# Lo parts of twelve projection weight units made in the first feed-forward stage, kept in DRAM and loaded by both projection stages

## The chip, the core and the metric

The kernel runs on one core of a Trainium2 chip. A core has a matrix engine (TensorE, PE in the profile, with its weight loads as PEld), a vector engine (VectorE, DVE), a scalar engine with activation functions (ScalarE, ACT), a general engine (GpSimd, POOL) and a sync engine (SyncE, SP) that here only issues DMA transfers. Data is worked on in on-chip memory, matmuls write into PSUM banks, and weights come from DRAM. The metric is the device time of one execution in microseconds; lower is better. Before the change three runs gave 2329.94 to 2330.9 us, with a median of 2329.94 us.

## What is computed

The reference is a two-layer decoder trunk over 528 positions (16 learned ones and 512 tokens) of width 1024, in float32. Only the first layer's mixer matters to the change:

```python
h = h + 0.5 * swiglu(rms_norm(h, g[0]), ffn_w_in[i, 0], ffn_w_out[i, 0])
hn = rms_norm(h, g[1])
h = h + rwkv7_time_mix(hn, ...)        # layer 0; layer 1 has sparse attention here
h = h + 0.5 * swiglu(rms_norm(h, g[2]), ffn_w_in[i, 1], ffn_w_out[i, 1])

def rwkv7_time_mix(h, mix, w_r, w_k, w_v, ...):
    xx = jnp.pad(h, ((0, 0), (1, 0), (0, 0)))[:, :-1] - h
    xm = h[None] + xx[None] * mix[:, None, None, :]
    xr, xw, xk, xv, xa, xg = xm[0], xm[1], xm[2], xm[3], xm[4], xm[5]
    r = xr @ w_r
    k = xk @ w_k
    v = xv @ w_v
    w_log = -jax.nn.softplus(-(w0 + jnp.tanh(xw @ w1) @ w2)) - 0.5
    a = jax.nn.sigmoid(a0 + (xa @ a1) @ a2)
    ...
```

So each projection multiplies its own mix of the normed input with that of the position before it.

## The kernel before

**Split products.** Every large product is made of three matmuls on rounded operands (`mm3`): a weight block and an input are each split into a hi part (rounded to the matmul's format) and a lo part (the rest), and hi by hi, hi by lo and lo by hi are added up in PSUM.

**Weights.** All weight blocks (128 by 128, and some wider) lie in DRAM in one array, `wall`, in the order of their use, packed in units of up to 1024 columns, eight blocks. The class `Weights` streams them. For each unit SP loads 512 KB into one of four `wraw` buffers, ScalarE makes the hi part (`whi`, by an activation that copies and rounds), and VectorE makes the lo part (`wlo`, by `tensor_sub` of raw and hi, called a split below). There are four buffers each of `wraw`, `whi` and `wlo`. `take` hands a block to the matmul code; at each call it first calls `split` for the unit two ahead, and in the second half of a unit it calls `round` for the unit three ahead. `prefetch` does the same from other places. One order of calls in the code is the order on each engine's queue, which is worked off in that order.

**Stages.** Positions are worked on in two ranges, A (0 to 272, padded to 288 in the mixer) and B (272 to 528). `STAGES` lists the order of the weights, and with it of the stages: feed-forward A (the first stage), projection A, feed-forward B, output projection A, projection B, and so on. A weight matrix used for both ranges is streamed twice, so both projection stages load the same units and split them anew. In the first stage 67 units are used.

**The projection stage.** `proj` makes mixes: for each of six uses i and eight channel blocks d, VectorE makes `tb` = hn + xx * mix, ScalarE rounds it into `xm_hi`, GpSimd subtracts it from `tb` into `xm_lo`. For the first use (i = 2, the k projection) VectorE also normalizes the block (`ynat`), takes the difference with the position before (`bu`), and, in range A only, copies the last position into `hnlast` for range B. There are four `tb` buffers (shared with other code) and twelve pairs of `xm_hi` and `xm_lo`. The order of matmuls is that of `proj_steps`: a first pass of `wk` over all d into four PSUM banks (32 blocks), a second pass for the other four banks with the sixteen blocks of the two low-rank factors (`lw`, `la`) among them, then `wv` and `wr`. The mixes are issued in the order k, w, a, v, r, g, each as soon as a buffer is free in program order. `evac` copies a finished bank to `BKV`. The first twelve units of the stage hold `wk`, `lw`, `la` and the first sixteen blocks of `wv`.

**Work beside.** The recurrence of the mixer (preparation, inverse, scan) runs as chains of small operations that a static planner, `run` with the prices of the class `Clock`, threads between the main matmuls. Its decisions are made when the program is built.

Of the kernel before, what the change touches and what calls it, by code (L numbers as in the profile page):

```python
# [10 lines left out]
F32 = mybir.dt.float32  # L11
F32R = mybir.dt.float32r
I32 = mybir.dt.int32
AF = mybir.ActivationFunctionType
# [120 lines left out]
def ao_blocks():  # L135
    return [blk("ao", d, m) for m in range(DT) for d in range(DT)]


STAGES = (("ffn", 0, 0), ("proj",), ("ffn", 0, 0), ("out",), ("proj",), ("ffn", 0, 1), ("out",), ("ffn", 1, 0),
          ("ffn", 0, 1, (0, 2)), ("idx",), ("ffn", 0, 1, (2, 4)), ("kvq",), ("ffn", 1, 0), ("ao",), ("idx",), ("kvq",),  # L140
          ("ffn", 1, 1), ("ao",), ("ffn", 1, 1))


def plan(stages=STAGES):


    f = {"ffn": ffn_blocks, "proj": proj_blocks, "out": out_blocks, "idx": idx_blocks, "kvq": kvq_blocks,
         "ao": ao_blocks}
    units, width = [], 0
    for name, *args in stages:  # L150
        for piece in f[name](*args):
            w = piece[3] - piece[2]
            if not units or width + w > (512 if len(units) < 3 else 1024):
                units.append([])
                width = 0
            units[-1].append((piece, width))
            width += w
    return units


def unit_width(u):
    (_, _, c0, c1), at = u[-1]
    return at + c1 - c0


def pack(units, mats):

    wall, c = np.empty(128 * sum(unit_width(u) for u in units), np.float32), 0
    for u in units:
        w = unit_width(u)  # L170
        t = wall[c:c + 128 * w].reshape(128, w)
        for (key, k, c0, c1), at in u:
            t[:, at:at + c1 - c0] = mats[key][k * 128:(k + 1) * 128, c0:c1]
        c += 128 * w
    return wall


class Weights:


    def __init__(self, nc, pool, wall, units, raw_bufs, bufs, ahead):
        self.nc, self.pool, self.wall, self.units = nc, pool, wall, units
        self.raw_bufs, self.bufs, self.ahead = raw_bufs, bufs, ahead
        self.flat = [(u, p) for u, unit in enumerate(units) for p in unit]
        self.start = 128 * np.concatenate([[0], np.cumsum([unit_width(u) for u in units])])
        self.pos = self.nraw = self.nhi = self.nlo = 0
        self.raw, self.hi, self.lo = {}, {}, {}

    def load(self):

# [20 lines left out]
    def split(self, last):  # L211

        while self.nlo <= min(last, len(self.units) - 1):
            self.round(self.nlo)
            r = self.raw.pop(self.nlo)
            w = r.shape[1]
            lo = self.pool.tile([128, 1024], F32R, name="wlo", bufs=self.bufs)
            self.nc.vector.tensor_sub(lo[:, :w], r, self.hi[self.nlo][:, :w].bitcast(F32))
            self.lo[self.nlo] = lo
            self.nlo += 1  # L220

    def prefetch(self, n):

# [3 lines left out]
    def take(self, piece):  # L227
        u, (p, at) = self.flat[self.pos]
        assert p == piece, (self.pos, p, piece)
        self.split(u + self.ahead)  # L230
        if at >= 512:
            self.round(u + self.ahead + 1)
        self.pos += 1
        s = slice(at, at + piece[3] - piece[2])
        return self.hi[u][:, s], self.lo[u][:, s]
# [195 lines left out]


@with_exitstack
def trunk(ctx, tc, wall, units, h0, vec, cstd, gqk, out, stop=None, gap=0.0, share=400.0, slack=200.0, fulls={}):
    clock = Clock()
    nc = Core(tc.nc, clock)
    @contextmanager
# [11 lines left out]
    W = Weights(nc, wpool, wall, units, raw_bufs=4, bufs=4, ahead=2)  # L449

    h = consts.tile([128, DT, T], F32, name="h")

# [12 lines left out]
    cst = {}  # L465
# [331 lines left out]
    hnlast = consts.tile([128, DT, 1], F32, name="hnlast")  # L797
# [4 lines left out]
    def proj(R, norm, sp, core, XB):  # L802

        r, n, pad, nch = R.r, R.n, R.pad, R.nch
        n0 = n - pad
        hn2 = [core.tile([128, 4, 1 + 288], F32, name="ynat", bufs=2) for _ in range(2)]
        hn = [hn2[d // 4][:, d % 4] for d in range(DT)]
# [5 lines left out]
                nc.vector.tensor_copy(hn2[i][:, :, 0:1], hnlast[:, 4 * i:4 * i + 4])  # L813
        if r not in norm.rstd:
            spread = norm.stat(r)
            W.prefetch(1)
            spread()
        xx = [core.tile([128, 4, 288], F32, name="bu", bufs=2) for _ in range(2)]
        if pad:
# [24 lines left out]
        def mixes(k):  # L844
            while k and queue and free[0]:
                i, d = queue.pop(0)
                if i == 2:
                    norm.apply(d, r, hn[d][:, 1:1 + n0])
                    nc.vector.tensor_sub(xx[d // 4][:, d % 4, :n0], hn[d][:, 0:n0], hn[d][:, 1:1 + n0])
                mix(i, d)  # L850
                if i == 2 and pad:
                    nc.vector.tensor_copy(hnlast[:, d], hn[d][:, n0:n0 + 1])
                free[0] -= 1
                k -= 1

# [55 lines left out]
        for kind, *st in proj_steps():  # L911
            if kind == "d":
# [15 lines left out]
            elif kind == "lora":  # L928
                key, d = st
# [13 lines left out]
            else:  # L943
                d = st[0]
# [906 lines left out]
```

## Time and profile before

| what | value |
|---|---|
| median of three runs | 2329.94 us |
| span of the profiled execution | 2326.1 us |
| instructions | 49383 |
| busy share of the span: PE, DVE, ACT, POOL | 97%, 73%, 54%, 8% |
| chain that ended last: PE, DVE, ACT, issue, DMA | 82%, 12%, 3%, 2%, 1% |
| splits (`wlo`) | 658 of 1235 ns mean |
| roundings of weights (`whi`) | 658 of 1051 ns mean |
| bytes moved | 355.98 MB, mean 153 GB/s |

The runs give device time alone; the profiled execution is one further execution, whose span from the first to the last instruction is 2326.1 us, 3.84 us less than the median of the runs. All rows name line 341, since a helper records every operation, so rows are told apart by their tiles: `acc<-xm_hi,whi` is a matmul of a mix with a weight's hi part into an `acc` bank. In the rows of a timeline the first number is the start in us, the second the busy time, a trailing xN says that N instructions in a row were merged, and a bracket says how long the engine was idle before and what ended that.

The first stage runs to about 212 us, projection A starts its matmuls at 221 us, and projection B its mixes at 660 us.

### The profile page before, as it was taken

What the parts mean: (1) busy time and instruction counts of PE and PEld (TensorE: products, weight loads), DVE (VectorE), ACT (ScalarE), POOL (GpSimd) and SP (SyncE); (2) the same over time, 40 slices, a digit from 0 to 9 for tenths busy, and PEclk for the clock granted to TensorE, in tenths of its full rate; (3) what the DMA queues carried; (4) which work ended last, traced back from release to release, by engine and by line L of the source; (5) the groups of instructions that cost most, each with busy time, mean ns of one, the idle gap of its engine ahead of it and who ended that gap; (6) DMA issues with size and microseconds to landing.
All of it is one profiled execution on the core that took longest, in us unless ns stands there. A gap on an engine that the chain in (4) does not pass through costs nothing.

```text
span 2326.1 us, 49383 instructions
## 1 busy us (share of the span) xinstructions
PE 2252.8 (97%) x20106; PEld 2171.0 (93%) x20106; DVE 1702.0 (73%) x3283; ACT 1264.8 (54%) x2137; POOL 174.5 (8%) x226
## 2 busy tenths in 40 slices
PE   8998899999989999999999999999999999999999
PEld 8998889998988899998999999989999899989999
DVE  7666888856887976577565757887656997876665
ACT  5444664466447634655444545457754647675543
POOL 0001521010033111000000000000000000000000
PEclk9999999999989999999999999999999999999999
DMA  6553334532434445234555555444454553434554
GB/s 233 177 172 124 128 128 152 193 113 66 146 128 145 156 153 166 83 128 149 182 172 173 181 166 181 162 160 149 137 182 148 168 175 117 151 109 156 185 183 144
DMA packets 101555, 355.98 MB, mean 153 GB/s; under 512 B 11552, under 2 KB 15728, under 8 KB 101328
## 3 DMA queue, kind: packets, MB, share of 16 engines
q1 hardware_dynamic: 99120, 347.91, 45.8%
q0 software_dynamic: 2208, 4.92, 0.8%
q8 instruction: 158, 2.59, 0.5%
q14 instruction: 69, 0.57, 0.1%
HBM read 348.51 MB, written 4.28 MB: 152 GB/s over the span
## 4 chain that ended last, share of the span: by engine, by line
PE 82%; DVE 12%; ACT 3%; issue 2%; DMA 1%; POOL 0%; SPq 0%; DVEq 0%; ACTq 0%; POOLq 0%
PE acc L341 70%; PE bg L341 8%; PE ry L341 3%; DVE wlo L341 3%; DVE tb L341 2%; ACT whi L341 1%; DMA wraw<-wall 1%; DVE ynat L341 0%; DVE rel L341 0%; DVE st L341 0%; DVE h L341 0%; DVE m L341 0%; DVE bu L341 0%; DVE pr L341 0%; DVE nst L341 0%
## 5 line engine op out<-in xcount | busy, mean ns | idle before, releaser
L341 ACT ACTIVATE whi<-wraw 128x1024 fp32r<-128x1024 f32 (+1 forms) x658 | 688.6, 1051 | 425.9 <-PE acc L341 272.0
L341 DVE TENSOR_TENSOR wlo<-wraw,whi 128x1024 fp32r<-128x1024 f32 (+1 forms) x658 | 810.5, 1235 | 148.8 <-ACT whi L341 147.9
L341 PE MATMUL acc<-hid_hi,whi 128*128 128x256 f32 (+1 forms) x1408 | 409.1, 291 | 4.6 <-DVE h L341 3.5
L341 PE MATMUL acc<-hid_lo,whi 128*128 128x256 f32 (+1 forms) x1408 | 399.9, 284 | 0.8 <-DVE hid_lo L341 0.8
L341 PE MATMUL acc<-hid_hi,wlo 128*128 128x256 f32 (+1 forms) x1408 | 400.0, 284 | 0.0
L341 PE MATMUL acc<-xa_hi,whi 128*128 128x256 f32 (+1 forms) x1088 | 310.6, 285 | 1.9 <-ACT xa_hi L341 1.9
L341 PE MATMUL acc<-xa_hi,wlo 128*128 128x256 f32 (+1 forms) x1088 | 309.0, 284 | 2.7 <-DVE wlo L341 2.7
L341 PE MATMUL acc<-x_hi,whi 128*128 128x272 f32 (+1 forms) x1024 | 302.8, 296 | 8.4 <-ACT whi L341 6.4
L341 PE MATMUL acc<-xa_lo,whi 128*128 128x256 f32 (+1 forms) x1088 | 308.2, 283 | 0.1
L341 PE MATMUL acc<-x_hi,wlo 128*128 128x272 f32 (+1 forms) x1024 | 294.6, 288 | 0.4 <-DVE wlo L341 0.4
L341 PE MATMUL acc<-x_lo,whi 128*128 128x272 f32 (+1 forms) x1024 | 294.2, 287 | 0.0
L341 PEld LDWEIGHTS acc<-hid_hi,whi 128*128 128x128 f32 x1408 | 265.7, 189 | 9.9 <-issue 4.3
L341 PEld LDWEIGHTS acc<-hid_lo,whi 128*128 128x128 f32 x1408 | 267.1, 190 | 1.3 <-DVE hid_lo L341 1.2
L341 PEld LDWEIGHTS acc<-hid_hi,wlo 128*128 128x128 f32 x1408 | 266.0, 189 | 0.0
L341 PE MATMUL acc<-xb_hi,whi 128*128 128x256 f32 x752 | 214.0, 285 | 0.0
L341 PE MATMUL acc<-xb_hi,wlo 128*128 128x256 f32 x752 | 211.3, 281 | 0.0
L341 PE MATMUL acc<-xb_lo,whi 128*128 128x256 f32 x752 | 211.3, 281 | 0.0
L341 PEld LDWEIGHTS acc<-xa_hi,wlo 128*128 128x128 f32 x1088 | 205.6, 189 | 3.8 <-DVE wlo L341 3.8
L341 PEld LDWEIGHTS acc<-xa_hi,whi 128*128 128x128 f32 x1088 | 205.8, 189 | 3.2 <-ACT xa_hi L341 2.1
L341 PEld LDWEIGHTS acc<-x_hi,whi 128*128 128x128 f32 x1024 | 195.1, 191 | 14.1 <-ACT whi L341 6.4
L341 PEld LDWEIGHTS acc<-xa_lo,whi 128*128 128x128 f32 x1088 | 205.8, 189 | 0.3 <-DVE xa_lo L341 0.3
L341 PEld LDWEIGHTS acc<-x_hi,wlo 128*128 128x128 f32 x1024 | 194.9, 190 | 1.0 <-DVE wlo L341 1.0
(309 smaller groups left out, 4376.5 us busy)
## 6 DMA issues: line engine op xcount, KB each, us to landing
wraw<-wall SPq DMA_DIRECT2D x643, 512.0 KB, 3.4
wraw<-wall SPq DMA_DIRECT2D x10, 438.0 KB, 3.3
out<-h SPq DMA_DIRECT2D x8, 256.0 KB, 2.3
h<-h SPq DMA_DIRECT2D x2, 512.0 KB, 7.9
ynat<-L POOLq DMA_DIRECT2D x2, 512.0 KB, 4.4
T<-ynat POOLq DMA_DIRECT2D x2, 512.0 KB, 4.8
gm<-T POOLq DMA_DIRECT2D x4, 224.0 KB, 7.0
L<-gm POOLq DMA_DIRECT2D x12, 64.0 KB, 2.1
```

Of the source, the lines that this page charges most:

```text
L341: r = f(*args, **kw)
```

## The change

`plan` now also gives an order of units with kinds. From the ninth unit of the first stage on (index 8), behind every fourth unit, one of the first twelve units of the projection is put in, of kind "save": it is loaded, rounded and split like any other, no matmul uses it, and its lo part is stored to a DRAM tile. In both projection stages the first twelve units are of kind "again": raw is loaded and rounded as before, but VectorE makes no split; SP loads the stored lo part into a `wlo` buffer instead. `back` issues these loads, three units ahead of the unit in use. While a save unit is among the next three, `take` looks one unit further ahead. Units are made to begin with the projection stage and to end with it.

Two smaller edits are in `proj`. `prefetch` at the head of projection A reaches three units ahead instead of one. The eight copies of the last position, by VectorE for each d, become two copies by ScalarE for four d each.

```diff
+SAVED, SAVE_FROM, SAVE_EVERY = 12, 8, 4
@@ plan
+    saved = {p + i: i for p in projs for i in range(SAVED)}
+    order, early = [], 0
+    for u, unit in enumerate(units):
+        order.append((u, "again" if u in saved else "use", saved.get(u)))
+        if early < SAVED and u >= SAVE_FROM and (u - SAVE_FROM) % SAVE_EVERY == 0:
+            order.append((projs[0] + early, "save", early))
+            early += 1
@@ split
-            self.round(self.nlo)
-            r = self.raw.pop(self.nlo)
+            u = self.nlo
+            self.round(u)
+            self.back(u)
+            r = self.raw.pop(u)
             w = r.shape[1]
-            lo = self.pool.tile([128, 1024], F32R, name="wlo", bufs=self.bufs)
-            self.nc.vector.tensor_sub(lo[:, :w], r, self.hi[self.nlo][:, :w].bitcast(F32))
-            self.lo[self.nlo] = lo
+            if self.kind[u] != "again":
+                lo = self.pool.tile([128, 1024], F32R, name="wlo", bufs=self.bufs)
+                self.nc.vector.tensor_sub(lo[:, :w], r, self.hi[u][:, :w].bitcast(F32))
+                self.lo[u] = lo
+            if self.kind[u] == "save":
+                d = self.saved[self.key[u]] = self.dram.tile([128, 1024], F32, name=f"lo{self.key[u]}")
+                self.nc.sync.dma_start(d, lo.bitcast(F32))
             self.nlo += 1
+
+    def back(self, last):
+
+        for u in range(self.nback, min(last + 1, len(self.units))):
+            if self.kind[u] == "again":
+                self.lo[u] = self.pool.tile([128, 1024], F32R, name="wlo", bufs=self.bufs)
+                self.nc.sync.dma_start(self.lo[u].bitcast(F32), self.saved[self.key[u]])
+            elif u > self.nlo:
+                return
+            self.nback = u + 1
@@ take
-        self.split(u + self.ahead)
+        n = self.ahead + ("save" in self.kind[u + 1:u + 4])
+        self.split(u + n)
+        self.back(u + 3)
         if at >= 512:
-            self.round(u + self.ahead + 1)
+            self.round(u + n + 1)
@@ proj
-            W.prefetch(1)
+            W.prefetch(3)
@@ mixes
-                if i == 2 and pad:
-                    nc.vector.tensor_copy(hnlast[:, d], hn[d][:, n0:n0 + 1])
+                if i == 2 and pad and d % 4 == 3:
+                    nc.scalar.activation(hnlast[:, d - 3:d + 1], hn2[d // 4][:, :, n0:n0 + 1], AF.Copy)
```

On VectorE, at the start of projection A, this stood before, from the normed block of d = 3 to the mix of d = 4:

```order
L341 SCALAR_TENSOR_TENSOR ynat<-h,vecs,rstd 128x272
L341 TENSOR_TENSOR bu<-ynat 128x272
L341 SCALAR_TENSOR_TENSOR tb<-bu,vecs,ynat 128x288
L341 COPY hnlast<-ynat 128x1
L341 TENSOR_TENSOR wlo<-wraw,whi 128x1024
L341 SCALAR_TENSOR_TENSOR ynat<-h,vecs,rstd 128x272
L341 TENSOR_TENSOR bu<-ynat 128x272
L341 SCALAR_TENSOR_TENSOR tb<-bu,vecs,ynat 128x288
```

Now it reads as follows from d = 6 to the end of the twelve units; the mixes of all later uses up to the low-rank result (llo) are one row of 29, the eighth mix of the first use among them:

```order
L376 SCALAR_TENSOR_TENSOR ynat<-h,vecs,rstd 128x272
L376 TENSOR_TENSOR bu<-ynat 128x272
L376 SCALAR_TENSOR_TENSOR tb<-bu,vecs,ynat 128x288
L376 SCALAR_TENSOR_TENSOR ynat<-h,vecs,rstd 128x272
L376 TENSOR_TENSOR bu<-ynat 128x272
L376 SCALAR_TENSOR_TENSOR tb<-bu,vecs,ynat 128x288 x29
L376 TENSOR_TENSOR llo<-ta,lhi 128x288
L376 TENSOR_TENSOR wlo<-wraw,whi 128x1024 x2
```

No split and no hnlast copy is left there; the order of the mixes among themselves is what it was. The same holds for projection B.

On SP, where before only raw loads stood (76 in a row, up to the constant `prod` of the preparation), the raw loads and the loads of stored lo parts now take turns around the start of projection A (the names lo_N are the DRAM tiles, in order of the units):

```order
L376 DMA wraw<-wall 128x1024 x14
L376 DMA wlo<-lo_380 128x1024
L376 DMA wraw<-wall 128x1024
L376 DMA wlo<-lo_575 128x1024
L376 DMA wraw<-wall 128x1024
L376 DMA wlo<-lo_730 128x1024
L376 DMA wraw<-wall 128x1024 x2
L376 DMA wlo<-lo_868 128x1024
L376 DMA wlo<-lo_1010 128x1024
L376 DMA wraw<-wall 128x1024
L376 DMA wlo<-lo_1158 128x1024
L376 DMA wraw<-wall 128x1024
```

The first three lo loads stand in the queue ahead of the last raw loads that the first stage issues.

On VectorE in the first stage, at the eviction of its first four banks (ta and tb from acc), this stood before:

```order
L341 TENSOR_TENSOR ss<-ss,tb 128x256
L341 TENSOR_TENSOR wlo<-wraw,whi 128x1024
L341 TENSOR_TENSOR ss<-ss,tb 128x256
L341 TENSOR_TENSOR ta<-acc,rstd 128x272
L341 TENSOR_TENSOR tb<-acc,rstd 128x272
```

and now this, with the first of the twelve added splits ahead of the eviction:

```order
L376 TENSOR_TENSOR ss<-ss,tb 128x256
L376 TENSOR_TENSOR wlo<-wraw,whi 128x1024 x2
L376 TENSOR_TENSOR ss<-ss,tb 128x256
L376 TENSOR_TENSOR ta<-acc,rstd 128x272
L376 TENSOR_TENSOR tb<-acc,rstd 128x272
```

More of the change, by code (lines that the diff above doesn't have):

```diff
@@ L148, in plan @@
          "ao": ao_blocks}
-    units, width = [], 0
+    units, width, projs = [], 1024, []
     for name, *args in stages:
+        if name == "proj":
+            projs.append(len(units))
+            width = 1024
         for piece in f[name](*args):
@@ L157, in plan @@
             width += w
-    return units
+        if name == "proj":
+            width = 1024
+    saved = {p + i: i for p in projs for i in range(SAVED)}
[5 more added lines that the diff above has]
+            early += 1
+    assert early == SAVED and order[-1][0] == len(units) - 1
+    return units, order
 def unit_width(u):
@@ L178, with __init__ @@
 class Weights:
-    def __init__(self, nc, pool, wall, units, raw_bufs, bufs, ahead):
-        self.nc, self.pool, self.wall, self.units = nc, pool, wall, units
+    def __init__(self, nc, pool, dram, wall, plan, raw_bufs, bufs, ahead):
+        units, order = plan
+        self.nc, self.pool, self.dram, self.wall = nc, pool, dram, wall
+        self.units, self.kind, self.key = [units[u] for u, _, _ in order], [o[1] for o in order], [o[2] for o in order]
         self.raw_bufs, self.bufs, self.ahead = raw_bufs, bufs, ahead
[L184 to L187, printed above, removed]
+        self.flat = [(i, p) for i, unit in enumerate(self.units) if self.kind[i] != "save" for p in unit]
+        start = 128 * np.concatenate([[0], np.cumsum([unit_width(u) for u in units])])
+        self.start = [start[u] for u, _, _ in order]
+        self.pos = self.nraw = self.nhi = self.nlo = self.nback = 0
+        self.raw, self.hi, self.lo, self.saved = {}, {}, {}, {}
     def load(self):
@@ L433, in trunk @@
 @with_exitstack
-def trunk(ctx, tc, wall, units, h0, vec, cstd, gqk, out, stop=None, gap=0.0, share=400.0, slack=200.0, fulls={}):
+def trunk(ctx, tc, wall, plan, h0, vec, cstd, gqk, out, stop=None, gap=0.0, share=400.0, slack=200.0, fulls={}):
     clock = Clock()
@@ L447, in trunk @@
     ctx.enter_context(tc.manual_schedule())
-    W = Weights(nc, wpool, wall, units, raw_bufs=4, bufs=4, ahead=2)
+    W = Weights(nc, wpool, dram, wall, plan, raw_bufs=4, bufs=4, ahead=2)
     h = consts.tile([128, DT, T], F32, name="h")
@@ L1840 @@
     arrays, mats = lay_out(inputs)
-    units = plan()
-    arrays["wall"] = pack(units, mats)
+    p = plan()
+    arrays["wall"] = pack(p[0], mats)
     nc = bacc.Bacc("TRN2", target_bir_lowering=False, num_devices=1)
@@ L1846 @@
     with tile.TileContext(nc) as tc:
-        trunk(tc, ap["wall"], units, ap["h0"], ap["vec"], ap["cst"], ap["gqk"], out)
+        trunk(tc, ap["wall"], p, ap["h0"], ap["vec"], ap["cst"], ap["gqk"], out)
     r = run_bass_kernel_spmd(nc, [arrays], core_ids=[0])
```

## The prediction

> **What bounds the kernel now.** I read the time by stretches first, for the share of TensorE, then TensorE's waits in the stretches where its count of matmuls falls, then the engines' rows in order of time there. In the rows below the columns are the stretch, its length, and for each engine its busy time with the number of instructions; then the granted clock, the DMA share and GB/s.
>
> ```profile
> 10.00:20.00 10.00, 9.84 (x76) 9.62 (x76) 7.86 (x12) 7.80 (x16) 0.00 (x0) 1.00 1.05 397
> 100.00:110.00 10.00, 10.00 (x82) 10.00 (x81) 6.44 (x11) 4.48 (x6) 0.00 (x0) 1.00 0.57 188
> 220.00:230.00 10.00, 8.53 (x49) 8.05 (x49) 9.62 (x21) 3.17 (x6) 4.45 (x4) 0.73 0.15 47
> 230.00:240.00 10.00, 6.86 (x37) 5.52 (x37) 9.62 (x17) 4.40 (x8) 5.41 (x5) 0.95 0.29 96
> 240.00:250.00 10.00, 10.00 (x69) 10.00 (x68) 10.00 (x11) 6.45 (x13) 7.75 (x8) 0.88 0.53 173
> 250.00:260.00 10.00, 9.66 (x72) 9.42 (x71) 10.00 (x9) 5.27 (x10) 9.75 (x9) 1.00 0.14 52
> 260.00:270.00 10.00, 5.91 (x35) 5.67 (x34) 9.45 (x11) 6.49 (x15) 7.43 (x8) 0.83 0.47 157
> 430.00:440.00 10.00, 10.00 (x87) 10.00 (x87) 9.53 (x18) 4.22 (x7) 0.00 (x0) 1.00 0.65 210
> 690.00:700.00 10.00, 10.00 (x86) 10.00 (x86) 10.00 (x11) 6.26 (x12) 9.64 (x10) 1.00 0.24 82
> 700.00:710.00 10.00, 5.55 (x35) 5.34 (x35) 8.91 (x11) 5.93 (x14) 7.79 (x9) 0.83 0.40 131
> ```
>
> In a feed-forward stage (430) TensorE is full and sets the time, though VectorE is busy for 9.53 of 10 us. In the first part of both projection stages (220 to 270, and up to 710) it is the other way round: the count falls to between 35 and 49 matmuls in four of these stretches, at a clock of 0.73 to 0.95, while VectorE is at 8.9 to 10. TensorE's real pace is read from the full rows: 72 matmuls in 9.66 us is 0.134 us in projection A, 86 in 10 is 0.116 us in projection B.
>
> Its waits, in the first stage (212 to 285 us) and then the second (590 to 735 us):
>
> ```profile
> PE acc L341 <- ACT BKV L341: 4.1, 1, 4.1
> PE acc L341 <- POOL xm_lo L341: 3.2, 5, 1.0
> ```
>
> ```profile
> PE acc L341 <- ACT BKV L341: 4.5, 1, 4.5
> ```
>
> It hardly waits for a lo part of the weights. It waits for mixed inputs (xm_lo), and once in each stage for ScalarE to empty the four banks of the second `wk` pass, which the first `wv` step needs. That eviction stands behind 29 rounded mixes (xm_hi) in ScalarE's order. So the chain is: VectorE makes a mix (tb), ScalarE rounds it, GpSimd subtracts; the four tb buffers come free when GpSimd is done. The splits delay that chain; that is how they cost time.
>
> **What the change takes from projection A.** VectorE in order of time, two splits among mixes:
>
> ```profile
> 226.18 1.21 DVE L341 TENSOR_TENSOR wlo<-wraw,whi 128x1024 fp32r<-128x1024 f32 x1
> 227.31 1.05 DVE L341 SCALAR_TENSOR_TENSOR ynat<-h,vecs,rstd 128x272 f32<-128x272 f32 x1
> ...
> 245.95 5.01 DVE L341 SCALAR_TENSOR_TENSOR tb<-bu,vecs,ynat 128x288 f32<-128x288 f32 x5
> 250.88 1.83 DVE L341 TENSOR_TENSOR wlo<-wraw,whi 128x1024 fp32r<-128x1024 f32 x1
> 252.64 5.06 DVE L341 SCALAR_TENSOR_TENSOR tb<-bu,vecs,ynat 128x288 f32<-128x288 f32 x5
> ```
>
> ```profile
> L341 DVE COPY hnlast<-ynat 128x1 f32<-128x1 f32 x8 | 1.1, 143 | 0.0
> ```
>
> A split takes 227.31 - 226.18 = 1.13 us of VectorE. GpSimd's first and eighth subtraction, the latter beside a split:
>
> ```profile
> 220.99 1.04 POOL L341 TENSOR_TENSOR xm_lo<-tb,xm_hi 128x288 fp32r<-128x288 f32 x1 [215.30 <-ACT xm_hi L341]
> ...
> 237.10 1.29 POOL L341 TENSOR_TENSOR xm_lo<-tb,xm_hi 128x288 fp32r<-128x288 f32 x1 [0.87 <-ACT xm_hi L341]
> ```
>
> First eight mixes: two splits stand ahead of the eighth, 2.3 us; of the eight hnlast copies I count 0.3 of 1.1 us, since neighbours overlap; the eighth subtraction loses its company, 0.25. It ends at 238.4 - 2.9 = 235.5 us. The two hnlast instructions that ScalarE gets instead hide in its idle time (3.17 busy of 10).
>
> The next 21 mixes: from 245.95 to 252.64, five mixes and one split took 6.69 us; without the split 5.55, or 1.11 a mix. I keep that pace, in which VectorE and GpSimd still slow each other; GpSimd's own 1.04 is the other end, worth 1.2 us over 17 mixes. Twelve mixes fit the buffers. TensorE has 22 matmuls left after the eighth, then 24 of the second pass before the first buffers come free: 235.5 + 46 x 0.134 = 241.7, while subtraction 12 ends at 239.9. With 0.4 for a rounding that is a gap of 2.2. Subtraction 25 ends at 235.5 + 17 x 1.11 + 2.2 = 256.6; its buffer takes mix 29, 1.0 us, at 257.6. Then ScalarE's row:
>
> ```profile
> 265.06 0.44 ACT L341 ACTIVATE xm_hi<-tb 128x288 fp32r<-128x288 f32 x1 [0.52 <-DVE tb L341]
> 265.41 1.04 ACT L341 ACTIVATE whi<-wraw 128x1024 fp32r<-128x1024 f32 x1
> 266.36 1.29 ACT L341 ACTIVATE BKV<-acc 128x288 f32<-128x288 f32 x4
> ```
>
> ```profile
> 266.80 0.61 PE L341 MATMUL acc<-xm_hi,whi 128*128 128x288 f32 x1 [4.09 <-ACT BKV L341]
> ...
> 267.93 0.45 PE L341 MATMUL acc<-xm_lo,whi 128*128 128x288 f32 x1
> 268.17 0.45 PE L341 MATMUL acc<-xm_hi,wlo 128*128 128x288 f32 x1
> ```
>
> From rounding 29 to the first `wv` matmul passes 1.74 us, so that comes at 259.4 instead of 266.80: **7.4 us**. After the wait, twelve matmuls ran 0.24 us apart, at half pace; a short wait spares that, 12 x 0.106 = **1.3 us**. TensorE itself could begin at 238.4 + 144 x 0.134 = 257.7, so what comes after the split is TensorE's own pace, and the stage can gain 9.1 + 1.3 = 10.4 at most. At least it keeps the 2.9 of the first eight. I take **8.7**.
>
> **Projection B**, the same steps (VectorE, GpSimd, TensorE):
>
> ```profile
> 666.94 1.21 DVE L341 TENSOR_TENSOR wlo<-wraw,whi 128x1024 fp32r<-128x1024 f32 x1
> ...
> 671.74 1.21 DVE L341 TENSOR_TENSOR wlo<-wraw,whi 128x1024 fp32r<-128x1024 f32 x1
> ...
> 687.95 4.50 DVE L341 SCALAR_TENSOR_TENSOR tb<-bu,vecs,ynat 128x256 f32<-128x256 f32 x5
> 692.37 1.76 DVE L341 TENSOR_TENSOR wlo<-wraw,whi 128x1024 fp32r<-128x1024 f32 x1
> 694.05 4.00 DVE L341 SCALAR_TENSOR_TENSOR tb<-bu,vecs,ynat 128x256 f32<-128x256 f32 x5
> ```
>
> ```profile
> 679.22 1.19 POOL L341 TENSOR_TENSOR xm_lo<-tb,xm_hi 128x256 fp32r<-128x256 f32 x1 [0.81 <-ACT xm_hi L341]
> ```
>
> ```profile
> 707.09 0.58 PE L341 MATMUL acc<-xm_hi,whi 128*128 128x256 f32 x1 [4.45 <-ACT BKV L341]
> ```
>
> Two splits ahead of the eighth mix, 2.3, and 0.25: subtraction eight ends at 680.4 - 2.5 = 677.9. The cycle from 687.95 to 694.05 is 6.10, less 1.13 is 0.99 a mix. TensorE is through its next 46 matmuls at 683.2, subtraction 12 at 681.9, gap 1.7; subtraction 25 ends at 677.9 + 16.8 + 1.7 = 696.4; mix 29 0.9; then 1.74: 699.0, a gain of **8.1 us**. The norm's statistics of the other half stay between the sixth and seventh mix and may leave a half-paced spell, so I add none for the clock. The floor, 680.5 + 144 x 0.116 = 697.2, allows 9.9 + 1.2 = 11.1; at least 2.5 stays.
>
> **What it adds.** In the first stage twelve whole units: 12 splits of 1.13 us (13.6 of VectorE), 12 roundings of about 1.0, 12 loads, 12 stores. The cover is TensorE, which the row at 430 shows full beside a VectorE at 9.53; the first stage shows 6.44 at 100 us, and 13.6 over its 190 us adds 0.7 per 10. One place is uncovered, the first added split, put ahead of the eviction of the first four banks:
>
> ```profile
> 28.65 0.43 DVE L341 TENSOR_TENSOR ta<-acc,rstd 128x272 f32<-128x272 f32 x1
> ```
>
> ```profile
> 29.66 6.01 PE acc L341 x48
> ```
>
> TensorE's chain goes on at 29.66; the eviction ends at 29.08, so 0.58 is spare of 1.13: a loss of **0.6 us**. Later, ScalarE's rounding of a unit ahead must wait for a whi buffer until the running unit is done, half a unit (12 matmuls at 82 in 10 us, some 1.5 us); what is queued behind it, a Silu or a hid rounding, is due only a unit later. If that cover fails, 12 saves cost 12 x 1.5 = 18.
>
> Each load of a lo part waits on SP for TensorE to leave the buffer, and the raw loads queue behind it; each raw load waits for ScalarE.
>
> ```profile
> wraw<-wall SPq DMA_DIRECT2D x643, 512.0 KB, 3.4
> out<-h SPq DMA_DIRECT2D x8, 256.0 KB, 2.3
> ```
>
> A lo load is issued three units ahead, 3 x 24 x 0.116 = 8.4 us in B, and takes 3.4 alone; stores, of which only half the size is shown, I put between 2.3 and twice that, and the buffer is wanted four units later. So none is on the path. What is needed is two loads per unit, 1.049 MB in 2.78 us, 377 GB/s in B and 326 in A; the row at 10 us moved 397. The Trainium skill's page "DMA: Bandwidth & Descriptors", under Specifications, puts one core's share of HBM at about 358 GB/s, which speaks against the change. By it a unit of B takes 2.93 us and the sum loses some 12 x 0.15 = 1.8 us; the 397 here is above it, so I leave that out.
>
> **Sum.** 8.7 + 8.1 - 0.6 = 16.2 us. What follows both places is TensorE at full count or chains that start from the stage's end, in nearly the same order, so the whole shifts. The profiled execution's span is 2326.1; the median of the runs is 2329.94, 3.84 around it. 2326.1 - 16.2 = 2309.9, and with 3.84 it is **2313.7, say 2314 us**.
>
> **Rivals.** (a) The forecast, chance 0.62. (b) TensorE at its floor in both stages: 10.4 + 11.1 = 21.5, 2308 us, chance 0.14. For it: GpSimd takes 1.04 beside a mix. Against: two engines in lockstep seldom leave none idle. A mechanism that leads near it is a split holding GpSimd off for its whole length: nine splits ahead of the eviction give 9 x 1.13 = 10.2 in each stage, 2310. The Trainium skill, "SBUF — State Buffer", under "SBUF: two separate sides", says that VectorE with two SBUF inputs and GpSimd take turns for whole instructions; by that rule it would be this. The trace agrees in part: the split beside GpSimd grew from 1.21 to 1.83. (c) ScalarE becomes the bound: it has 18.2 us of work between 240 and 270 and would have to do most of it in 20. If it holds the eviction back, only the first eight mixes gain: 2.9 + 2.5 less 0.6, 2325 us, chance 0.12. (d) The shift is lost before the end in a chain that the shift doesn't move: 2329, chance 0.06; against it, the scan starts from the stage's results. (e) Slower: the lo loads come late. At R GB/s a unit takes 1049/R us; eight units per stage can't be preloaded. At 232 GB/s, say, that is 4.5, against 3.2 and 2.8: 8 x 1.3 + 8 x 1.7 = 24 lost, 2338 us. It outweighs the gain below 8 x (2 x 1049/R - 6.0) = 16.2, R = 262. Against it: 397 with queues full. Chance 0.06. That the change doesn't do what it says is ruled out by the order: all 24 splits are gone from the two stages, 12 stand in the first.
>
> The range, 2307 to 2325, spans the floors and the least gains above and leaves out (d), (e) and part of (c). This kernel's measurement tells 0.2%, 4.7 us, from no change: faster 0.86, within it 0.08, slower 0.06.
>
> **What would show it.** Right: 60 or more matmuls in each 10 us after the start of the mixes, BKV waits under 2 us, first `wv` matmul some 8 us sooner in both, POOL near 10 of 10, and TensorE unbroken in the first stage but for 0.6 us near 30. Wrong: waits for wlo on a DMA, whi roundings that run into each other before the eviction, or a gain in a stage that is given back before the next.

## The result and the profile after

| | before | after |
|---|---|---|
| median of the runs (4 and 4) | 2329.94 us | 2313.14 us |
| lowest to highest | 2329.67 to 2330.9 us | 2311.55 to 2314.16 us |
| span of the profiled execution | 2326.1 us | 2309.8 us |
| ratio of the times, 95% interval | | 0.9927, 0.9913 to 0.9941 |

The changed kernel is 16.8 us faster; 16.2 had been predicted, and the predicted time of 2314 us is 0.9 us off. The total is right. Its terms are less so, and the runs below show why.

The page of the changed kernel, its span and the busy time of each engine with its share and its instructions:

```profile
span 2309.8 us, 49453 instructions
...
PE 2244.9 (97%) x20106; PEld 2164.9 (94%) x20106; DVE 1685.5 (73%) x3263; ACT 1275.2 (55%) x2151; POOL 163.5 (7%) x226
```

The two projection stages by stretches, in the columns of the prediction:

```profile
220.00:230.00 10.00, 7.40 (x42) 7.08 (x43) 9.38 (x17) 2.41 (x6) 4.34 (x5) 0.70 0.10 32
230.00:240.00 10.00, 9.08 (x63) 8.35 (x62) 8.09 (x13) 6.83 (x15) 5.46 (x6) 1.00 0.82 283
240.00:250.00 10.00, 10.00 (x77) 10.00 (x76) 7.59 (x9) 7.28 (x15) 9.01 (x10) 1.00 0.86 296
250.00:260.00 10.00, 10.00 (x77) 10.00 (x76) 9.68 (x11) 7.13 (x17) 9.55 (x11) 1.00 0.77 279
260.00:270.00 10.00, 8.95 (x70) 8.01 (x69) 8.01 (x8) 9.63 (x18) 4.63 (x6) 1.00 0.24 75
680.00:690.00 10.00, 9.53 (x82) 9.33 (x81) 10.00 (x13) 7.16 (x15) 10.00 (x12) 1.00 0.85 315
690.00:700.00 10.00, 8.74 (x72) 8.19 (x74) 7.78 (x10) 9.93 (x21) 5.15 (x7) 1.00 0.26 76
```

From 230 us on TensorE does 63 to 77 matmuls in each 10 us of projection A, where 35 to 72 stood before, and 82 and 72 in the two stretches of B; the granted clock is 1.00 in all of them. VectorE is no longer busy throughout, and GpSimd is close to it in the longest rows of mixes (9.55 and 10.00). The lo loads show in the last column, with up to 315 GB/s in these rows.

GpSimd in order of time: one subtraction with VectorE at rest, and the long unbroken rows of the two stages:

```profile
240.08 0.81 POOL L376 TENSOR_TENSOR xm_lo<-tb,xm_hi 128x288 fp32r<-128x288 f32 x1 [1.69 <-ACT xm_hi L376]
...
242.61 16.33 POOL L376 TENSOR_TENSOR xm_lo<-tb,xm_hi 128x288 fp32r<-128x288 f32 x17 [0.44 <-ACT xm_hi L376]
...
674.76 15.78 POOL L376 TENSOR_TENSOR xm_lo<-tb,xm_hi 128x256 fp32r<-128x256 f32 x18 [0.52 <-ACT xm_hi L376]
```

That is 16.33 / 17 = 0.96 us a mix in projection A and 15.78 / 18 = 0.88 in B; the prediction had 1.11 and 0.99. TensorE at the first `wv` matmul (`acc<-xm_hi,whi`) of each stage:

```profile
258.20 0.30 PE L376 MATMUL ry<-xm_hi,wlo 128*128 128x288 f32 x1
258.34 0.30 PE L376 MATMUL acc<-xm_hi,whi 128*128 128x288 f32 x1
...
689.97 0.39 PE L376 MATMUL acc<-xm_hi,whi 128*128 128x256 f32 x1 [0.47 <-ACT BKV L376]
```

In A it follows the matmul before it in 0.14 us, with no wait at all: TensorE is at its own pace, which the prediction had called the floor. In B 0.47 us of the wait for `BKV` are left of 4.45. Waits of TensorE in the first stage (0 to 215 us):

```profile
PE acc L376 <- ACT whi L376: 6.2, 1, 6.2
PE bg L376 <- DVE ss L376: 1.1, 2, 0.9
PE acc L376 <- DVE ta L376: 0.6, 1, 0.6
PE acc L376 <- DVE wlo L376: 0.2, 1, 0.2
```

The wait for ta, 0.6 us near 30 us, is the one that was predicted there. Before, the first of these rows was 6.4 us and the row for ta was missing.

**Where the time went.** Five stretches add up to the span: up to the first subtraction (xm_lo) of projection A, from there to its low-rank result (llo), on to the first subtraction of projection B, to its llo, and to the end. Differences of the starts of these rows between a kernel's trace and that of before (for the changed kernel 222.17, 263.98, 654.56, 695.45 and 2309.8, against 220.99, 272.98, 662.49, 713.14 and 2326.1) give this table; minus is time saved. It holds all runs of the next section too.

| kernel | first stage | projection A | between | projection B | behind | span |
|---|---|---|---|---|---|---|
| the changed kernel | +1.18 | -10.18 | +1.07 | -9.76 | +1.39 | -16.3 |
| two small edits alone | -0.19 | -3.06 | +1.55 | -0.12 | -0.58 | -2.4 |
| prefetch alone | +0.20 | -2.64 | +0.87 | -0.11 | -0.42 | -2.1 |
| saves, lo parts not used | +1.06 | -3.11 | +1.22 | -0.16 | -0.51 | -1.5 |
| needless subtraction | +0.83 | -3.11 | +0.85 | -0.13 | -0.04 | -1.6 |
| needless maximum | +2.58 | -8.52 | +0.50 | -4.88 | -9.78 | -20.1 |
| first projection alone | +0.62 | -10.17 | +0.71 | -0.16 | -1.10 | -10.1 |
| eight units | +0.86 | -5.78 | +0.18 | -5.13 | -0.33 | -10.2 |
| first save later | -0.09 | -10.22 | -0.26 | -9.34 | -1.59 | -21.5 |
| nine late units too | +3.49 | -10.22 | -0.14 | -9.42 | +2.99 | -13.3 |
| buffers 32 bytes on | +1.56 | -10.23 | -0.04 | -9.73 | -12.06 | -30.5 |
| the same, first save later | +0.95 | -10.26 | -0.28 | -9.56 | -15.45 | -34.6 |
| buffers 64 bytes on | +0.88 | -10.23 | +2.22 | -9.76 | -4.51 | -21.4 |

Unlike the medians, the columns compare single executions. The projection columns repeat wherever a stage is left alike, within 0.1 us in A and 0.4 in B; the others scatter by more. The column between the stages, for one, runs from -0.28 to +2.22 among the five kernels that differ from each other only in the first save or in where buffers lie.

### The profile page after: what moved, and what is told of

It is laid out like the page before. It is cut to its first block, busy times and chain, and to the rows that moved or that the text cites. A ratio compares the mean times of both kernels' runs of the same rounds, so it can differ in the third digit from the quotient of the medians.

```text
span 2309.8 us, 49453 instructions
## 1 busy us (share of the span) xinstructions
PE 2244.9 (97%) x20106; PEld 2164.9 (94%) x20106; DVE 1685.5 (73%) x3263; ACT 1275.2 (55%) x2151; POOL 163.5 (7%) x226
## 4 chain that ended last, share of the span: by engine, by line
PE 81%; DVE 12%; ACT 4%; issue 2%; DMA 1%; POOL 0%; SPq 0%; ACTq 0%; DVEq 0%; POOLq 0%
PE acc L376 70%; PE bg L376 8%; PE ry L376 3%; DVE wlo L376 3%; DVE tb L376 2%; ACT whi L376 1%; DMA wraw<-wall 1%; DVE rel L376 1%; DVE m L376 0%; DVE st L376 0%; DVE h L376 0%; DVE bu L376 0%; DVE ynat L376 0%; DVE nst L376 0%; DVE pr L376 0%
## 5 line engine op out<-in xcount | busy, mean ns | idle before, releaser
L376 ACT ACTIVATE whi<-wraw 128x1024 fp32r<-128x1024 f32 (+3 forms) x670 | 701.0, 1051 | 421.6 <-PE acc L376 273.7
L376 DVE TENSOR_TENSOR wlo<-wraw,whi 128x1024 fp32r<-128x1024 f32 (+1 forms) x646 | 791.9, 1229 | 168.9 <-ACT whi L376 158.0
```

The costliest lines, as they stand in the source:

```text
L376: r = f(*args, **kw)
```

## The experiments

The theory after the two traces: a split costs its time between the mixes, on VectorE and on GpSimd beside it, and that alone is what the change removes. Rivals: VectorE's occupation alone, the small edits, the loads and stores.

**The saves without their use, and the two small edits.**

```diff
-        order.append((u, "again" if u in saved else "use", saved.get(u)))
+        order.append((u, "use", None))
```

> The twelve save units are loaded, rounded, split and stored in the first stage, and both projection stages make their own splits as before. This prices the first stage alone. Theory (the added units hide behind a full TensorE but for the start of the stage): the end of the first stage comes 1.2 us later, as in the changed kernel, nothing is won or lost later, and the time is about 2331 us (2330 to 2332). Rival (the small edits, the earlier prefetch and the copies moved to ScalarE, carry part of the gain): below 2328. Rival (the saves also cost something that the gain hides in the changed kernel): above 2333.

Measured: 2326.69 us against 2328.43 us for the kernel before on the same chip, ratio 0.9992 (0.9983 to 1.0001). The theory's 2331 is missed and its first rival, below 2328, holds: something in it wins. The next run shows what.

```diff
-SAVED, SAVE_FROM, SAVE_EVERY = 12, 8, 4
+SAVED, SAVE_FROM, SAVE_EVERY = 0, 8, 4
```

> No unit is saved; only the two small edits stand (the earlier prefetch at the head of projection A, the copies of the last position on ScalarE). Theory: within 1 us of the kernel before, 2329 to 2330 us. Rival (they carry part of the gain): below 2327.

Measured: 2326.04 against 2328.81, ratio 0.9987 (0.9978 to 0.9996). The theory was wrong here: the two edits bring 3.06 us, all in projection A. VectorE in this kernel ahead of the first mix:

```profile
215.65 0.35 DVE L376 SCALAR_TENSOR_TENSOR nst<-nst 68x4 f32<-68x4 f32 x2
215.92 2.35 DVE L376 TENSOR_TENSOR wlo<-wraw,whi 128x1024 fp32r<-128x1024 f32 x2
218.56 0.50 DVE L376 SCALAR_TENSOR_TENSOR ynat<-h,vecs,rstd 128x272 f32<-128x272 f32 x1 [0.29 <-ACT rstd L376]
```

Two splits that stood between the mixes (at 226.18 and 231.36 us before) now run at 215.92, while VectorE would have waited for the norm's statistics: only 0.29 us of that wait are left. To part the two edits:

```diff
-                if i == 2 and pad and d % 4 == 3:
-                    nc.scalar.activation(hnlast[:, d - 3:d + 1], hn2[d // 4][:, :, n0:n0 + 1], AF.Copy)
+                if i == 2 and pad:
+                    nc.vector.tensor_copy(hnlast[:, d], hn[d][:, n0:n0 + 1])
```

(with no saves, as above)

> Of the whole change only the earlier prefetch at the head of projection A; the last position is copied by VectorE as before. Theory: two splits move from between the mixes into the wait for the norm's statistics ahead of the first mix, which brings 2 to 3 us in projection A, and the time is 2326 to 2328 us, so most of what the two small edits brought together (ratio 0.9987). Rival (the copies moved to ScalarE brought it): no change, 2329 us or more.

Measured: 2326.78 against 2330.1, ratio 0.9987 (0.9978 to 0.9995). The prefetch alone brings 2.64 us of the stage, as expected, so the copies are left with 3.06 - 2.64 = 0.4. This is what the prefetch is worth without the saves. In the changed kernel the two splits that it moves are among those that are gone, so the two gains are in part the same; no run has the saves without the prefetch, and what it adds to them isn't shown. Projection B has no such prefetch and gains 9.76 us. The saves themselves cost some 1.2 us of the first stage, which the table has at -0.19 without and at +1.06 with them.

**A needless subtraction in place of each removed split.** Everything of the change stands, all loads of lo parts too; the reference is computed in full, and the added operation's result is used by nobody.

```diff
+            if self.kind[u] == "again":
+                self.nc.vector.tensor_sub(r, r, self.hi[u][:, :w].bitcast(F32))
```

> The changed kernel, with a needless subtraction on VectorE in place of each of the 24 removed splits (raw minus hi, written over raw, whose result nobody uses). It has the length and the two inputs of a split. Theory (the splits' time on VectorE, between the mixes, is all that the change removed): the first wv matmuls come 7 to 10 us later again in each stage and the time goes back to 2330 to 2332 us. Rival (the gain comes from something else, such as the two small edits): stays below 2322.

Measured: 2326.63 against 2328.43, ratio 0.9992 (0.9983 to 1.0001), the same as the saves without use (2326.69 on the same chip). It is below the expected 2330 to 2332 by what the small edits bring. So the whole gain beyond the edits, 7.1 us in A and 9.6 in B, is the splits' absence, and the loads of lo parts cost nothing that can be measured.

**A needless maximum at the same place**, whose one large input is the raw weights; otherwise as before, and the reference is computed in full.

```diff
+            if self.kind[u] == "again":
+                m8 = self.pool.tile([128, 8], F32, name="wm8", bufs=1)
+                self.nc.vector.max(m8, r)
```

> As the run with the needless subtraction, but with a needless maximum over the raw weights, an operation with one large input and an output of eight numbers. If VectorE's occupation is what costs, the time is that of the needless subtraction (2330 to 2332), as far as the durations are alike. If it is what a two-input operation takes from GpSimd, GpSimd's rows keep the pace of the changed kernel (0.96 and 0.88 us a mix) beside the maximum and at least half of the gain stays: 2322 or less.

Measured: 2305.91 against 2328.43, ratio 0.9904 (0.9891 to 0.9918). That is even below the changed kernel, by 9.78 us won behind projection B, which the last three runs take up. They also show that the added buffer by itself leaves the two stages as they are (-10.23 and -9.73). The stages decide here. Groups of instructions by form between 243 and 262 us (busy time, mean ns of one, idle time before them), with the subtraction:

```profile
L378 POOL TENSOR_TENSOR xm_lo<-tb,xm_hi 128x288 fp32r<-128x288 f32 x15 | 17.5, 1195 | 2.1 <-ACT xm_hi L378 2.1
L378 DVE SCALAR_TENSOR_TENSOR tb<-bu,vecs,ynat 128x288 f32<-128x288 f32 x16 | 13.9, 925 | 0.0
L378 DVE TENSOR_TENSOR wraw<-wraw,whi 128x1024 f32<-128x1024 f32 x4 | 7.3, 1820 | 0.0
```

and with the maximum:

```profile
L379 POOL TENSOR_TENSOR xm_lo<-tb,xm_hi 128x288 fp32r<-128x288 f32 x18 | 16.7, 953 | 2.3 <-ACT xm_hi L379 2.3
L379 DVE SCALAR_TENSOR_TENSOR tb<-bu,vecs,ynat 128x288 f32<-128x288 f32 x18 | 14.2, 844 | 0.0
...
L379 DVE MAX8 wm<-wraw 128x8 f32<-128x1024 f32 x5 | 6.1, 1215 | 0.0
```

Begun while GpSimd is idle, the two take the same time, 1.21 and 1.22 us. Begun while GpSimd works, as here, the subtraction takes 1.82 and GpSimd's own operation 1.20; the maximum stays at 1.22, and GpSimd at 0.95, about its pace in the changed kernel; a subtraction of GpSimd that runs wholly beside a maximum (at 248.72 us) takes 0.81, as with VectorE at rest. TensorE's wait for `BKV` in projection A is 5.6 us with the subtraction and 1.7 with the maximum. So with VectorE taken up for 1.22 us at each of these places, but not held longer, projection A keeps 8.52 - 3.1 = 5.4 of 7.1 us. Projection B keeps 4.88 - 0.1 = 4.8 of 9.6. There two maxima stand among the first eight mixes, which follow each other with no slack, and TensorE waits for the seventh:

```profile
671.39 0.58 PE L379 MATMUL acc<-xm_hi,whi 128*128 128x256 f32 x1 [2.38 <-ACT xm_hi L379]
```

```profile
672.00:677.00 5.00, 4.62 (x21) 4.62 (x22) 5.00 (x8) 3.01 (x7) 2.60 (x4) 0.50 0.44 160
```

Behind that wait stands a stretch (the second row, of the view by stretches) at a clock of 0.50, with 21 matmuls in 5 us where 45 are the pace at full clock. So VectorE's occupation is the smaller part in A and, with the slow spell that follows it, about half in B: the wait of 2.38 us and some 24 matmuls of 0.12 us too few are about the 4.9 us that are lost. The rest is what the subtraction and GpSimd take from each other. The maximum differs from the subtraction in two ways, one large input instead of two and 8 numbers written instead of 1024; no run parts these, so that it is the second input is argued here, not shown. The Trainium skill, "SBUF — State Buffer", under "SBUF: two separate sides", says that a VectorE instruction with two SBUF inputs and a GpSimd instruction that reads SBUF exclude each other for a whole instruction. These rows agree in kind (1.82 and 1.20 against 1.22 and 0.95). Read strictly, over the durations in the trace, they don't: in the changed kernel a mix, which has two inputs as well, and a subtraction pass in 0.96 us, while the subtraction alone takes 0.81 and the mix alone 0.52 (VectorE, next row), 1.33 in turns. Either the two overlap in part, or these durations hold more than the part that excludes the other; no run tells which.

```profile
240.93 0.52 DVE L376 SCALAR_TENSOR_TENSOR tb<-bu,vecs,ynat 128x288 f32<-128x288 f32 x1 [1.78 <-POOL xm_lo L376]
```

**One projection, or fewer units.**

```diff
-    saved = {p + i: i for p in projs for i in range(SAVED)}
+    saved = {p + i: i for p in projs[:1] for i in range(SAVED)}
```

> Only the first projection stage loads stored lo parts; the second makes its twelve splits as before. Theory by the two traces: the first stage loses 1.2, projection A wins 10.2, a half-clock spell behind it gives 1.3 back, so 7.7 of the gain stay and the time is 2322 us (2321 to 2324). By the terms of the prediction it would be 8.7 - 0.6 = 8.1, about the same. Rival (the shift of the first stage is lost before the end): 2328 or more.

Measured: 2317.82 against 2328.43, ratio 0.9956 (0.9944 to 0.9969), or 10.6 us won, where 2321 to 2324 us were expected. Projection A wins its 10.17 and B nothing, so the stages are independent, and nothing of A's gain is lost on the way. The loss behind A that the expectation counted with is +0.71 here. It is +0.85 to +1.55 in kernels that have no use of lo parts at all, and below zero in others that have it, so this column is scatter of single executions as far as the runs show.

```diff
-SAVED, SAVE_FROM, SAVE_EVERY = 12, 8, 4
+SAVED, SAVE_FROM, SAVE_EVERY = 8, 8, 4
```

> Eight units are saved instead of twelve. Theory (TensorE is at its floor in both projection stages, so the last splits are already covered): the time is that of the changed kernel within 1.5 us, 2312 to 2315. Rival (each split costs its time of VectorE, as in the prediction's sum): two thirds of the two stages' gain of 19.5 us, so 2329.9 - 13 + 1.2 + 1.3 = 2319 us.

Measured: 2318.55 against 2328.81, ratio 0.9952 (0.9939 to 0.9964). The rival's time was right, its reason less so. The last four units are worth 10.18 - 5.78 = 4.4 us in A and 4.6 in B, 1.1 a split; the first eight are worth 5.13 in B, 0.6 a split, and in A only 5.78 - 3.06 = 2.7 beyond the small edits. The two stages gained 10.9 us, less than the rival's two thirds of 19.5, and the columns outside them lost less than it had counted. With twelve units the wait for `BKV` is just gone in A and 0.47 us in B; whether eleven would do, no run shows.

**Moving the first save**, from index 8 to 12:

```diff
-SAVED, SAVE_FROM, SAVE_EVERY = 12, 8, 4
+SAVED, SAVE_FROM, SAVE_EVERY = 12, 12, 4
```

> The first saved unit is put in four units later, so that no added split stands ahead of the first eviction near 30 us. Theory of the prediction: the 0.6 us wait for ta near 30 us goes, and the time is 2312.5 us. Rival (the first stage's loss of 1.2 us has another source, the loads at its start): the end of the first stage stays where it is in the changed kernel, 212.86 us in its trace, and the time stays at 2313 us.

Measured: 2309.82 against 2328.81, ratio 0.9914 (0.99 to 0.9928). TensorE's waits in its first stage:

```profile
PE acc L376 <- ACT whi L376: 6.3, 1, 6.3
PE bg L376 <- DVE ss L376: 1.1, 2, 0.9
```

The wait for ta is gone, and the first stage ends where it did before (-0.09). From 14 to 44 us it loses nothing (-0.1), where the changed kernel loses 0.9. In the trace the theory holds; in the medians the interval overlaps that of the changed kernel, so that the 0.0013 between them isn't shown.

**Nine more units**, index 20 to 28, with a save behind every two or three units:

```diff
-SAVED, SAVE_FROM, SAVE_EVERY = 12, 8, 4
+SAVED, SAVE_FROM = [*range(12), *range(20, 29)], 12
+    slots = {SAVE_FROM + 5 * j // 2: i for j, i in enumerate(SAVED)}
```

> Nine more units are saved and loaded back, those of the end of the projection (index 20 to 28), where TensorE waits for the last mixes in both kernels, with a save behind every two or three units of the first stage. Theory (that wait comes from the splits between the last mixes, and it starts the half-clock spell behind projection A): the wait goes, the spell with it, and 2 to 4 us more are won, 2309 to 2311 us. Rival (the wait comes from the buffers of the mixes or from ScalarE, and the first stage pays for nine more saves): 2313 to 2316 us.

Measured: 2313.66 against 2328.81, ratio 0.9935 (0.9922 to 0.9947). The theory was wrong, and the time is the rival's. TensorE's waits around the end of projection A (300 to 352 us), in this kernel:

```profile
PE acc L377 <- POOL xm_lo L377: 1.8, 1, 1.8
PE acc L377 <- ACT xm_hi L377: 1.8, 1, 1.8
```

and in the changed kernel:

```profile
PE acc L376 <- POOL xm_lo L376: 2.2, 1, 2.2
PE acc L376 <- ACT xm_hi L376: 1.3, 1, 1.3
```

3.6 against 3.5 us: the splits are not what the last mixes wait for. And the first stage ends 3.49 us late with its 21 saves, of which 1.1 are there before the first save; the saves cost 2.4.

**The second layer.** The maximum's run won 9.78 us behind projection B, where its order of work is that of the changed kernel. The one other difference was a buffer of 32 bytes in a partition, so three runs kept the buffer and left the maximum out:

```diff
+            if self.kind[u] == "again" and self.m8 is None:
+                self.m8 = self.pool.tile([128, 8], F32, name="wm8", bufs=1)
+                self.nc.vector.memset(self.m8, 0.0)
```

> The changed kernel with one more small buffer of 32 bytes in a partition, which is set to zero once and never used, so that buffers laid out behind it may lie elsewhere. It is the one thing besides the maximum itself that the run with one input had more than the changed kernel. In that run some 10 us were won far behind the projections, in the second layer, where the order of work is that of the changed kernel. Theory (where the buffers lie sets TensorE's pace there): the second layer wins about 10 us again, 2303 us. Rival (it came from the maximum's delay or from chance): 2311 to 2315 us.

Measured: 2297.43 against 2330.1, ratio 0.9858 (0.9843 to 0.9873). The gain behind B is 12.06 us, more than the 10 that were expected, so the buffer suffices for it.

> The same small buffer, with the first save four units later. Theory: 1 to 3 us below the run with the small buffer alone, by the first stage's loss of 1.2 us that goes; with the second layer's gain, if that comes from the buffer, about 2300 us. Rival (the gain of the later first save was chance): equal to the run with the small buffer alone.

Measured: 2298.18 against 2330.1 on the same chip, ratio 0.9861 (0.9848 to 0.9875). In the medians the rival holds: moving the first save changes nothing that can be measured, though the first stage again ends 0.6 us earlier in the trace.

> As the run with the small buffer, which here takes 64 bytes in a partition instead of 32, so that every buffer laid out behind it lies 64 bytes further than in the changed kernel. Theory (TensorE's pace in the second layer hangs on where its inputs lie within 64 bytes: at a multiple of 64 in the changed kernel, 32 beside it in the run with 32 bytes): the second layer is as slow as in the changed kernel, 2313 us (2310 to 2316). Rival (any shift moves the inputs away from a bad place, or the one instruction that sets the buffer matters): 2297 us again (2294 to 2301).

(with a buffer of `[128, 16]`.) Measured: 2307.46 against 2328.81, ratio 0.9911 (0.9894 to 0.9927). That lies in neither expected range. Most of the gain is gone, as the theory had it, and the interval overlaps that of the changed kernel; but -4.51 us behind B are more than the changed kernel's +1.39. The last feed-forward matmuls of the second layer, in order the changed kernel, 32 bytes on, 64 bytes on, and the maximum's run, whose buffers also lie 32 bytes on:

```profile
L376 PE MATMUL acc<-xa_hi,whi 128*128 128x256 f32 x304 | 85.8, 282 | 0.0
```

```profile
L380 PE MATMUL acc<-xa_hi,whi 128*128 128x256 f32 x304 | 83.9, 276 | 0.0
```

```profile
L380 PE MATMUL acc<-xa_hi,whi 128*128 128x256 f32 x304 | 85.4, 281 | 0.0
```

```profile
L379 PE MATMUL acc<-xa_hi,whi 128*128 128x256 f32 x304 | 85.4, 281 | 0.0
```

The first three speak for the place within 64 bytes and against the mere presence of the buffer. The fourth has the faster place and not the pace, so in this group the place isn't all. Earlier, all three kernels with 32 bytes agree. The main matmuls that run from 1307 to 1885 us in the kernel before take 6.6, 7.8 and (with the maximum) 7.3 us less there, with 64 bytes 1.2 less, and in the nine other kernels of the table between 0.4 less and 0.4 more.

## Why the prediction was right, and which terms were not

**The chain was the right one.** Splits delay the mixes, the mixes delay ScalarE's eviction of the `wk` banks, and that holds the first `wv` step. Operations of the same length and inputs, put in their place, took back everything but the edits' share, and the wait for `BKV` came back with them (5.6 and 5.2 us).

**Projection A, 8.7 predicted, 10.18 measured; projection B, 8.1 predicted, 9.76 measured.** By the parts of the prediction's sum, counted in both traces from the first subtraction to the end of the eighth (after: 236.21 and 669.96 us), to the first `wv` matmul, and to the low-rank result:

| us won | A, predicted | A, measured | B, predicted | B, measured |
|---|---|---|---|---|
| first eight mixes | 2.9 | 3.36 | 2.5 | 2.52 |
| from there to the first `wv` matmul | 4.5 | 6.28 | 5.6 | 6.67 |
| from there to the low-rank result | 1.3 | 0.54 | none | 0.57 |

The step that was mis-sized is the second, by its pace "without the split 5.55, or 1.11 a mix" and "6.10, less 1.13 is 0.99 a mix". A split's 1.13 us, from its start to that of the next operation, was read at 226.18, where GpSimd was idle as it began. The very rows quoted for the pace have it at 252.64 - 250.88 = 1.76 and 694.05 - 692.37 = 1.68; the first of these splits began 0.28 us into a subtraction on GpSimd (at 250.61). With these, (6.69 - 1.76) / 5 = 0.99 and (6.10 - 1.68) / 5 = 0.88, and 0.96 and 0.88 were measured. "GpSimd's own 1.04 is the other end" was wrong for the same reason: that row was itself beside VectorE, and alone the subtraction takes 0.81. With 0.99 and 0.88 the prediction's own steps put the first `wv` matmul at the floor in A and 0.5 us behind it in B, which is near its rival (b), and in B 0.47 us of the wait were left.

The third part was mis-sized the other way. In A the twelve half-paced matmuls are gone as predicted (they follow in 0.13 us now), but the low-rank result comes only 0.54 us nearer, and TensorE waits for its two parts (lhi 0.7 and llo 0.4 us, where llo 0.3 stood before).

**The small edits.** The earlier prefetch was given nothing. By itself it brings 2.64 us, by moving just the two splits that the prediction has removed from ahead of the eighth mix. With the copies as well, but without the saves, the first eight mixes end 3.12 us sooner, with the whole change 3.36, so in this part little is left for the saves to win. The hnlast copies were put at 0.3 and measure 0.4.

**First stage, 0.6 predicted, 1.18 measured.** The wait near 30 us is the predicted one. The trace calls 0.6 us of it idle, but from start to start TensorE loses 0.9 there: one matmul starts at 29.67 us, the next at 30.56 and the one after that at 30.80, where 0.13 lie between two otherwise. The four other kernels with a first save at index 8, the same buffers and nothing else in this stage lose 0.9 to 1.1 between 14 and 44 us. The remaining 0.3 are there by 11 us, ahead of the first added split, and scatter from -0.5 to +0.3 among the same kernels. The other eleven saves cost nothing: from 44 us to the end of the stage the changed kernel loses no more.

**Not predicted:** +1.07 us between the projections and +1.39 behind B. The former appears without the use of lo parts too and is missing in other kernels with it (scatter, as above). Of the latter some 1 us is real. TensorE from 695 to 760 us in the changed kernel:

```profile
PE bg L376 <- ACT gm L376: 1.3, 1, 1.3
PE bg L376 <- ACT lhi L376: 1.0, 1, 1.0
```

and before, at the same work (713 to 778 us):

```profile
PE bg L341 <- DVE llo L341: 0.4, 1, 0.4
PE bg L341 <- ACT lhi L341: 0.2, 1, 0.2
```

At 765 us of the kernel before, TensorE has lost 1.05 us in this stretch in the changed kernel, 0.9 to 1.3 in four others with the whole change (1.9 with nine more units), and less than 0.05 in the five that make their own splits in B or subtract needlessly. It seems that the preparation's chains through ScalarE don't come forward as far as the main matmuls do; no run took this apart. The rest of the column is scatter: it is -1.59 in the kernel with the first save later.

**The sum** came this near by luck: 3.1 us too little gain in the stages (19.94 against 16.8) meet 3.0 too little loss elsewhere (3.64 against 0.6), and part of that loss is the scatter of one execution. In the kernel with the first save later the three outer columns add up to -1.94. The 3.84 us "around" the span are no constant either: in the profiled execution of the changed kernel 2311.55 - 2309.8 = 1.75 lie around it. So the execution profiled before was some 2 us faster than its median; that of the changed kernel was 1.6 faster than its own, which is why the error did not show.

**The rivals.** (b) nearly holds inside the stages (19.94 of 21.5), but the rest of the kernel takes back 3.6 us in this execution. (c) ScalarE is at 9.63 and 9.93 in the stretch of the evictions, yet the wait for it fell from 4.1 to none and from 4.5 to 0.5. (d) fell with the run on the first projection alone, (e) with the needless subtraction: all loads of lo parts, and no loss. The loads came near the price that the prediction weighed, in the busiest 5 us of projection B of the changed kernel:

```profile
679.00:684.00 5.00, 5.00 (x45) 5.00 (x44) 5.00 (x7) 3.43 (x9) 5.00 (x7) 1.00 0.99 362
```

TensorE is full there at 362 GB/s. The Trainium skill, "DMA: Bandwidth & Descriptors", under Specifications, has about 358 GB/s as one core's limit. This row is above it, and nothing was lost to it here.

## What to carry to other kernels

An operation that is to be removed is worth its length in company, and what it adds to its neighbour, not its length alone: here 1.76 us rather than 1.13, and the difference decides whether the next engine reaches its floor. Small edits beside the main one need a price of their own, and a run of their own: one changed number, without the saves, moved two splits into an idle wait and won 2.6 us. A sum that comes out is no proof of its terms; compare them one by one over several executions. And a difference of this size may also come from where buffers lie, so a new or removed buffer ahead of the others is worth a run by itself.

## What was not expected of the hardware

At a granted clock of 1.00, with TensorE full and the same matmuls to do, its pace was not the same in all kernels, and in most places it went with where the buffers lie. In the second layer the 256-wide matmuls ran at 85 to 87 in 10 us in the changed kernel and at 88 to 91 with every buffer behind the weights 32 bytes further on. Two stretches of that kernel:

```profile
2180.00:2190.00 10.00, 10.00 (x91) 10.00 (x90) 7.26 (x12) 5.36 (x7) 0.00 (x0) 1.00 0.57 185
...
2210.00:2220.00 10.00, 10.00 (x91) 10.00 (x90) 5.44 (x9) 4.68 (x7) 0.00 (x0) 1.00 0.51 181
```

The same work in the changed kernel:

```profile
2190.00:2200.00 10.00, 10.00 (x86) 10.00 (x85) 6.78 (x11) 4.64 (x7) 0.00 (x0) 1.00 0.53 166
...
2220.00:2230.00 10.00, 10.00 (x86) 10.00 (x85) 5.49 (x9) 4.87 (x7) 0.00 (x0) 1.00 0.50 161
```

In the kernels as built, the inputs (xa_hi) lie at byte 102400 of a partition in the changed kernel, a multiple of 64, at 102432 in the faster one, and at 102464, a multiple of 64 again, where most of the gain is lost. The weight buffers, which lie ahead, are at 32 beside a multiple of 64 in all three. Over the whole execution the matmuls of another input (xb_hi) go with the place in all of these kernels, in order the changed kernel, 32 bytes on, the maximum's run (the same places), and 64 bytes on:

```profile
L376 PE MATMUL acc<-xb_hi,whi 128*128 128x256 f32 x752 | 213.9, 284 | 0.0
L380 PE MATMUL acc<-xb_hi,whi 128*128 128x256 f32 x752 | 212.1, 282 | 0.0
L379 PE MATMUL acc<-xb_hi,whi 128*128 128x256 f32 x752 | 211.6, 281 | 0.0
L380 PE MATMUL acc<-xb_hi,whi 128*128 128x256 f32 x752 | 214.0, 285 | 0.0
```

Two things don't fit the place of TensorE's inputs as the whole cause. The last group of the maximum's run stayed at 281 ns, as shown above. And in the first stage it goes the other way: from 44 to 194 us the three kernels with 32 bytes lose 0.3 us each, and the kernels without the buffer nothing, but for the one with nine more saves. The buffer moves everything behind the weights at once, so whether it is the place of the inputs itself, or that against the weights, or another buffer that VectorE, ScalarE or a transfer uses, stays open. The kernel before has the layout of the changed one; it was not tried with the shift. The fastest kernel of this study is the change with that buffer, 2297.43 us.
